# Hybrid decoder layer on one core: token-major x loaded later, 16 columns on another queue, one more filling matmul, and work of the scan and of the attention norm put off

## The chip, the core and the metric

The kernel runs on one core of one Trainium2 chip. The metric is device time in microseconds (us) of one launch. The engines are PE (TensorE: matmuls, and PEld for its weight loads), DVE (VectorE), ACT (ScalarE), POOL (GpSimd) and SP (SyncE, which issues transfers here). Each has its own instruction stream, which it works through in order; they wait for each other through semaphores. SP, ACT and POOL each issue transfers (DMA).

## The reference, cut to what matters

One layer over 256 tokens and a model width of 2048, in float32. `P` stands for the combined input projection.

```python
h = x + 0.5 * swiglu(rmsnorm(x, ffn1_norm), ffn1_w_gu, ffn1_w_down)        # d_ff 5632
P = rmsnorm(h, mix_norm) @ w_in                                            # u | v | z | x | B | C | dt
a = gelu(u) * (tril(w_s) @ rmsnorm(gelu(v)) + b)                           # gated mixing in chunks of 128
x, B, C = split(silu(causal_conv(xBC)));  dt = softplus(dt + dt_bias)
m = ssd_scan(x, dt, -exp(a_log), B, C) + d_skip * x                        # 32 heads of 64, 8 groups, chunk 128
m = rmsnorm(m * silu(z), ssm_norm)
h = h + concat([a, m]) @ w_out
h = h + cross_attention(rmsnorm(h, xa_norm), rmsnorm(mem, mem_norm))       # 4 heads, 256 memory tokens
h = h + 0.5 * swiglu(rmsnorm(h, ffn2_norm), ffn2_w_gu, ffn2_w_down)
out = rmsnorm(h, final_norm)
```

Inside a chunk the scan needs, for each head, `decay[l, s] = exp(cum[l] - cum[s])` for s ≤ l, multiplied by the scores `C @ B`, and that times `x * dt`. `cum` is the running sum of `dt * a`.

## The kernel before, in words

**Products.** Each weight matrix is read once, in pieces of 256 rows by 1024 columns (1 MB, tile `raw`, three buffers, issued by SP). A float32 product is made of three fp32r matmuls: ACT rounds the piece to `hi` (L168, or L190 in quarters for the very first pieces), DVE subtracts to get `lo` (L176), and PE multiplies hi by the activations' high part, lo by the high part and hi by the low part. An ordinary piece (kind C) is 24 matmuls of 128x512; a piece of kind S trades matmuls for sums of blocks (21 matmuls, with further DVE and ACT work). `hi` has three buffers and `lo` two, so `lo` of a piece can be written as soon as the piece two before it has been multiplied.

**Order.** PE's instructions stay in the order in which the program writes them. Other engines' instructions are placed by the framework's scheduler from that program. Side work is put in a list by `later(fn, by)` and runs at a step (L78 to L87): `step()` is called after each piece of weights (in two halves for pieces of kind C), and a job runs at the first step at or after its number, jobs of equal number in the order of the list.

**The start.** The first FFN needs x in two forms: turned (`xt`, features on partitions, tile `turned`, eight loads of 256 KB), which `x_operand` scales by the norm's weights (`col`, whose first 16 columns of 128x244 come early, L113) and splits into operands; and by tokens (`x`, tiles `h0` to `h3`, eight loads of 256 KB by `x_load`, L102), which is the residual stream and from which `Normed.stats` (L491) takes the sum of squares (ACT, `junk`). The factor 1/rms is needed only where the first column block's outputs are scaled (L564), since it scales rows. The first column block goes through its eight pieces in the order 0, 2, 4, 6, 1, 3, 5, 7 (`FIRST`). The pieces 0, 2 and 4 of weights are requested ahead of all, then the turned x, and by `x_operand` (L594) the tokens' x. `keep_busy(4)` puts matmuls on zeros ahead of the first real matmul.

**The scan.** In four parts (two chunks t, two halves j of the heads) `scan_start` (L808) issues the load of `cum` to all partitions (`dec`, 1 MB, POOL's queue) and at once puts down its use: subtraction (L820), minimum against a mask (L821), exponential on ACT (L822), the scores' matmuls, and the multiplication by the scores (L828). `scan_apply` (L832) multiplies by `x * dt` on PE (`yp`) and adds. The parts are called out at steps of the projection v, between its pieces (L875). All this shares twelve large buffers (`slot`).

**The attention norm.** While w_out is added to the stream, `Normed.chunk` puts off the turning of the new stream and the sums of squares (`stats`), the latter by 3 steps. The memory's norm and its turned form are loaded through POOL's queue (`prep_mem`, L966) at the start of w_q.

Of the kernel before, what the change touches and what calls it, by code (L numbers as in the profile page):

```python
# [38 lines left out]
C_FFN1, C_MIX, C_SSM, C_XA, C_MEM, C_FFN2 = (16 * i for i in range(6))  # L39
# [7 lines left out]
def hybrid_layer(ctx: ExitStack, tc: tile.TileContext, x, xt, mem, memt, w_gu1, w_dn1, w_in, w_s, w_out,  # L47
                 w_q, w_kv, w_o, w_gu2, w_dn2, cols, rows, gm_vn, fin, out):
    nc = tc.nc
# [22 lines left out]
    def matmul(out, lhsT, rhs, start=False, stop=False):  # L72
        return pe(nc.tensor.matmul(out, lhsT=lhsT, rhs=rhs, start=start, stop=stop))  # L73
# [4 lines left out]
    def later(fn, by=1):  # L78
        put_off.append((steps[0] + by, len(put_off), fn))
# [9 lines left out]
    def slot(shape, dtype, name):  # L89
        return big.tile(shape, dtype, name=name, tag="slot")  # L90

    def half_k(dtype, name):
        return tmp.tile([P, NC], dtype, name=name, tag="t2k")

    def side(name):
        return mm.tile([P, NC], F32, name=name, tag="bank")
# [5 lines left out]
    def x_load(i, queue=nc.sync):  # L102
        c = i * KP * P
        queue.dma_start(out=h[c // NC][:, :, c % NC:c % NC + KP * P], in_=x_v[:, :, c:c + KP * P])

    def turned_load(w, i, queue, to=None):
        to = half_k(F32, "turned").rearrange("p (k s) -> p k s", k=KP) if to is None else to
        queue.dma_start(out=to, in_=w[i * KP * P:(i + 1) * KP * P, :].rearrange("(k p) s -> p k s", p=P))
        return to

    x_turned = {0: turned_load(xt, 0, nc.scalar)}
    col = const.tile([P, N_COLS], F32, name="col")
    nc.scalar.dma_start(out=col[:, :C_MIX], in_=cols[:, :C_MIX])  # L113
    x_turned[2] = turned_load(xt, 2, nc.scalar)
    warm = const.tile([P, 1], F32, name="warm")
    nc.vector.memset(warm, 0.0)
# [272 lines left out]
    def operand_later(srcs, to, name, c0=None, by=1):  # L389
        def half(q):  # L390
            if q == 0:
                to.append(slot([P, KG, 2 * S], F32R, name))
            return to_operand(srcs, to[at], q, c0)

        at = len(to) + sum(1 for o in owed if o is to)
        owed.append(to)

        def first():
            owed.remove(to)
            assert len(to) == at  # L400
            half(0)
            later(lambda: half(2), by=0)

        later(first, by)
# [4 lines left out]
    class Pieces(dict):  # L409
        def __init__(self, kinds, name, donor=None):  # L410

            self.kinds, self.name, self.half, self.made, self.donor = kinds, name, None, {}, donor
# [57 lines left out]
    class Normed:  # L470


        def __init__(self, name, c0, kinds=None, bys=None):
            self.bys = bys
            self.name, self.c0 = name, c0
            self.xts = [] if kinds is None else Pieces(kinds, f"xp_{name}")
            self.ss = small.tile([P, NT, 4], F32, name=f"ss_{name}", bufs=1)

        def chunk(self, n, by=1):
            srcs = [h[n][:, t, :] for t in range(NT)]  # L480
            if isinstance(self.xts, Pieces):

                for i in (2 * n, 2 * n + 1):
                    later(lambda i=i: self.xts.put(i, srcs, i % 2 * KP, self.c0 + n * KG),
                          self.bys.get(i, by))
                later(lambda: self.stats(n), 3)
            else:
                operand_later(srcs, self.xts, f"xt_{self.name}{n}", self.c0 + n * KG, by)
                self.stats(n)
# [91 lines left out]
    n1 = Normed("ffn1", C_FFN1, GU_KINDS)  # L581
# [11 lines left out]

    def x_operand(i):  # L594
        n1.xts.put(i, x_turned.pop(i), i % 2 * KP, n1.c0 + i // 2 * KG)
        for j in {2: (5,), 4: (7,), 6: (0, 1), 1: (2, 3), 3: (4, 5), 5: (6, 7)}.get(i, ()):
            if j in (5, 7) and i in (2, 4):
                x_turned[j] = turned_load(xt, j, nc.sync)
            else:
                x_load(j)  # L600


    idle = const.tile([P, S], F32, name="idle")
# [2 lines left out]
    def keep_busy(n):  # L606
        ps = side("idle")
        for i in range(n):
            matmul(ps[:, :S], idle[:, :P], idle, start=True, stop=True)

    keep_busy(4)
    x_operand(0)
    for i, by in ((2, 0.5), (4, 1), (6, 1.5), (1, 2), (3, 2.5), (5, 3), (7, 3.5)):
        later(lambda i=i: x_operand(i), by=by)
    for n in range(4):
        later(lambda n=n: n1.stats(n), by=4 + n / 2)

    def late_loads():
        with behind(n1.xts.made[7]):
# [182 lines left out]
    def per_head(ap, n):  # L802
        return ap.unsqueeze(2).broadcast_to([P, ap.shape[1], n])
# [2 lines left out]
    scan = {}  # L806

    def scan_start(t, j):  # L808
        hs = slice(j * 16, j * 16 + 16)
        if j == 0:  # L810
            scan["xdt"] = scan[f"xdt{t}"] = xdt = slot([P, HEADS, HD], F32, "xdt")
            nc.vector.tensor_tensor(out=xdt, in0=y[t], in1=per_head(dt[:, t, :], HD), op=ALU.mult)
            nc.vector.tensor_tensor(out=y[t], in0=y[t], in1=per_head(rowb[:, 2, :], HD), op=ALU.mult)
        dec = slot([P, 16, P], F32, "dec")
        nc.gpsimd.dma_start(
            out=dec.rearrange("p h l -> p (h l)"),
            in_=cum_rows[t:t + 1, j * 16 * P:(j + 1) * 16 * P].broadcast_to([P, 16 * P]))
        if t == 0:
            nc.vector.tensor_tensor(out=dend[:, hs], in0=dec[:, :, P - 1], in1=cum[:, t, hs], op=ALU.subtract)
        nc.vector.tensor_tensor(out=dec, in0=dec, in1=per_head(cum[:, t, hs], P), op=ALU.subtract)  # L820
        nc.vector.tensor_tensor(out=dec, in0=dec, in1=lim.unsqueeze(1).broadcast_to([P, 16, P]), op=ALU.min)  # L821
        nc.scalar.activation(dec, dec, AF.Exp)  # L822
        sc = side("scores").rearrange("p (g l) -> p g l", l=P)
        for i in range(4):
            matmul(sc[:, i, :], bt[:, j * 4 + i, t * P:(t + 1) * P], ctr[:, j * 4 + i, t * P:(t + 1) * P],
                   start=True, stop=True)
        dec4 = dec.rearrange("p (g r) l -> p g r l", r=REP)
        nc.vector.tensor_tensor(out=dec4, in0=dec4, in1=sc.unsqueeze(2).broadcast_to([P, 4, REP, P]),  # L828
                                op=ALU.mult)
        scan["dec"] = dec  # L830

    def scan_apply(t, j):  # L832
        dec, xdt = scan["dec"], scan["xdt"]
        for q in range(2):
            yp = side("yp").rearrange("p (h d) -> p h d", d=HD)
            for i in range(8):
                hh = q * 8 + i
                matmul(yp[:, i, :], dec[:, hh, :], xdt[:, j * 16 + hh, :], start=True, stop=True)
            ys = y[t][:, j * 16 + q * 8:j * 16 + q * 8 + 8, :]
            nc.vector.tensor_tensor(out=ys, in0=yp, in1=ys, op=ALU.add)  # L840
        if j == 0:
            return
        if t == 0:
            nc.scalar.activation(dend, dend, AF.Exp)
            nc.vector.tensor_tensor(out=xdt, in0=xdt, in1=per_head(dend, HD), op=ALU.mult)
            later(scan_states, by=2)
        else:
            for q in range(4):
                yo = side("yo")
                for i in range(2):  # L850
                    g = q * 2 + i
                    matmul(yo[:, i * S:(i + 1) * S], ctr[:, g, P:], scan["states"][:, g, :], start=True, stop=True)
                tq = half_k(F32, "yoff").rearrange("p (h d) -> p h d", d=HD)
                nc.vector.tensor_tensor(out=tq, in0=yo.rearrange("p (h d) -> p h d", d=HD),
                                        in1=per_head(ecum[:, q * 8:q * 8 + 8], HD), op=ALU.mult)
                ys = y[t][:, q * 8:q * 8 + 8, :]
                nc.vector.tensor_tensor(out=ys, in0=ys, in1=tq, op=ALU.add)
# [14 lines left out]
                            base=0, channel_multiplier=-1)  # L872
    v = [slot([P, 4, NC], F32, f"v{t}") for t in range(NT)]
    ss_v = small.tile([P, NT, 4], F32, name="ss_v", bufs=1)
    for i, (by, to) in enumerate(((3, 7), (7, 10), (13, 17), (17, 21))):  # L875
        later(lambda i=i: scan_start(i // 2, i % 2), by=by)
        later(lambda i=i: scan_apply(i // 2, i % 2), by=to)
    for c in (0, 2):
# [69 lines left out]
    for c in range(4):  # L948
        later(lambda c=c: m_operand(c), by=1 + c)
    XA_KINDS = "CCCCCSCS"  # L950
    na = Normed("xa", C_XA, XA_KINDS, {4: 1, 6: 1, 5: 1.5, 7: 2})

    class Both:
        made = {}
# [203 lines left out]
```

## Time and profile before

| what | value |
|---|---|
| median of 3 runs | 2462.12 us (2462.08 to 2463.76) |
| the profiled execution's own time | 2464.31 us |
| its span in the profile | 2462.6 us |
| PE busy | 2442.9 us (99% of the span), 11363 matmuls |
| DVE busy | 2034.9 us (83%) |
| ACT busy | 1311.2 us (53%) |
| mean granted TensorE clock | 0.997 |
| read from memory | 476.76 MB, 194 GB/s over the span |

The profile is of one execution; its own time is 1.7 us above its span. A matmul row's end is modelled and overlaps the next one's start, so what matters on PE is from start to start, and the gap that a row shows in brackets with the engine and line that ended it. In rows of the timeline the columns are start and duration in us, engine, line, operation, output and inputs, shapes, how many; in brackets the idle time ahead of it and what ended that.

### The profile page before, as it was taken

What the parts mean: (1) busy time and instruction counts of PE and PEld (TensorE: products, weight loads), DVE (VectorE), ACT (ScalarE), POOL (GpSimd) and SP (SyncE); (2) the same over time, 40 slices, a digit from 0 to 9 for tenths busy, and PEclk for the clock granted to TensorE, in tenths of its full rate; (3) what the DMA queues carried; (4) which work ended last, traced back from release to release, by engine and by line L of the source; (5) the groups of instructions that cost most, each with busy time, mean ns of one, the idle gap of its engine ahead of it and who ended that gap; (6) DMA issues with size and microseconds to landing.
All of it is one profiled execution on the core that took longest, in us unless ns stands there. A gap on an engine that the chain in (4) does not pass through costs nothing.

```text
span 2462.6 us, 29086 instructions
## 1 busy us (share of the span) xinstructions
PE 2442.9 (99%) x11363; PEld 2035.3 (83%) x11363; DVE 2034.9 (83%) x1936; ACT 1311.2 (53%) x1218; POOL 28.5 (1%) x60
## 2 busy tenths in 40 slices
PE   8999999999999999999999999999999999999998
PEld 6888888888888888788888888888888888888887
DVE  6999889999877778655598888778889988899987
ACT  6555445555546554435555655555555544555554
POOL 0000000000000000000000100000000000000000
PEclk9999999999999999999999999999999999999999
DMA  8555665565656554545556665555555655655664
GB/s 276 188 205 189 205 205 198 197 204 188 205 180 212 193 179 169 198 158 187 184 197 227 222 201 171 171 177 182 188 195 198 205 191 203 205 189 205 200 210 154
DMA packets 202730, 480.80 MB, mean 195 GB/s; under 512 B 15696, under 2 KB 19824, under 8 KB 201824
## 3 DMA queue, kind: packets, MB, share of 16 engines
q1 hardware_dynamic: 199088, 466.41, 56.7%
q0 software_dynamic: 2528, 11.48, 1.3%
q8 instruction: 89, 1.46, 0.2%
q10 hardware_dynamic: 976, 1.06, 0.1%
q14 instruction: 49, 0.40, 0.0%
HBM read 476.76 MB, written 2.13 MB: 194 GB/s over the span
## 4 chain that ended last, share of the span: by engine, by line
PE 95%; issue 3%; ACT 1%; DVE 1%; DMA 0%; POOL 0%; ACTq 0%; SPq 0%; POOLq 0%; DVEq 0%
PE acc L73 91%; PE tpose L76 2%; PE yp L73 1%; PE logits L73 0%; PE o L73 0%; ACT hi L168 0%; DVE lo L176 0%; DMA raw<-in_w_gu 0%; DMA turned<-in_xt 0%; PE mixed L73 0%; ACT junk L352 0%; PE dt L73 0%; PE scores L73 0%; ACT mem L972 0%; PE yo L73 0%
## 5 line engine op out<-in xcount | busy, mean ns | idle before, releaser
L176 DVE TENSOR_TENSOR lo<-raw,hi 128x2048 fp32r<-128x2048 f32 (+2 forms) x446 | 944.5, 2119 | 280.0 <-PE acc L73 220.1
L168 ACT CAST hi<-raw 128x2048 fp32r<-128x2048 f32 (+1 forms) x438 | 787.5, 1799 | 538.0 <-PE acc L73 472.4
L73 PE MATMUL acc<-hi,xp_ffn 128*128 128x512 f32 x1824 | 581.9, 392 | 6.4 <-ACT hi L168 4.4
L73 PEld LDWEIGHTS acc<-hi,xp_ffn 128*128 128x128 f32 x1824 | 344.5, 189 | 78.6 <-ACT hi L168 4.8
L168 ACT CAST hi<-sum 128x2048 fp32r<-128x2048 f32 x117 | 224.3, 1917 | 300.6 <-PE acc L73 169.9
L73 PE MATMUL acc<-lo,xp_ffn 128*128 128x512 f32 x912 | 356.9, 391 | 1.5 <-DVE lo L176 1.5
L176 DVE TENSOR_TENSOR lo<-sum,hi 128x2048 fp32r<-128x2048 f32 x117 | 268.1, 2291 | 32.4 <-ACT hi L168 31.8
L73 PE MATMUL acc<-hi,hid 128*128 128x512 f32 x896 | 282.5, 390 | 0.0
L73 PE MATMUL acc<-hi,xt_mix 128*128 128x512 f32 x768 | 241.7, 393 | 0.0
L73 PEld LDWEIGHTS acc<-lo,xp_ffn 128*128 128x128 f32 x912 | 172.3, 189 | 37.6 <-DVE lo L176 2.5
L538 DVE TENSOR_TENSOR part<-acc,part 128x512 f32<-128x512 f32 x272 | 180.4, 685 | 24.6 <-ACT part L504 9.0
L73 PEld LDWEIGHTS acc<-hi,hid 128*128 128x128 f32 x896 | 168.2, 188 | 34.8
L73 PE MATMUL acc<-lo,hid 128*128 128x512 f32 x448 | 174.3, 389 | 0.0
L73 PEld LDWEIGHTS acc<-hi,xt_mix 128*128 128x128 f32 x768 | 144.2, 188 | 30.4 <-issue 0.7
L176 DVE TENSOR_TENSOR sum<-sum,raw 128x512 f32<-128x512 f32 x234 | 161.5, 690 | 6.6
L73 PE MATMUL acc<-lo,xt_mix 128*128 128x512 f32 x384 | 149.6, 390 | 1.1 <-DVE lo L176 1.1
L73 PE MATMUL acc<-hi,xp_ffn1s 128*128 128x512 f32 x466 | 148.5, 389 | 0.0
L73 PE MATMUL acc<-hi,xp_ffn2s 128*128 128x512 f32 x466 | 148.5, 389 | 0.0
L176 DVE TENSOR_TENSOR sum<-raw 128x1024 f32<-128x1024 f32 x117 | 142.4, 1217 | 0.0
L73 PE MATMUL acc<-xt_mix,hi 128*128 128x512 f32 x512 | 140.5, 396 | 0.0
L73 PE MATMUL acc<-hi,hids 128*128 128x512 f32 x392 | 125.2, 389 | 0.0
L73 PE MATMUL acc<-hi,memt 128*128 128x512 f32 x384 | 123.4, 392 | 0.0
(285 smaller groups left out, 3125.8 us busy)
## 6 DMA issues: line engine op xcount, KB each, us to landing
raw<-in_w_gu SPq DMA_DIRECT2D x286, 512.0 KB, 3.7
raw<-in_w_in SPq DMA_DIRECT2D x80, 1024.0 KB, 5.1
raw<-in_w_dn SPq DMA_DIRECT2D x60, 1024.0 KB, 5.2
raw<-in_w_gu SPq DMA_DIRECT2D x132, 256.0 KB, 3.9
raw<-in_w_kv SPq DMA_DIRECT2D x24, 1024.0 KB, 5.3
raw<-in_w_out SPq DMA_DIRECT2D x21, 1024.0 KB, 5.3
raw<-in_w_dn SPq DMA_DIRECT2D x28, 512.0 KB, 4.0
raw<-in_w_dn SPq DMA_DIRECT2D x56, 256.0 KB, 4.4
```

Source lines behind the costliest of these rows:

```text
L73: return pe(nc.tensor.matmul(out, lhsT=lhsT, rhs=rhs, start=start, stop=stop))
L76: return pe(nc.tensor.transpose(out=out, in_=in_, identity=identity))
L168: last_cast[:] = [nc.scalar.copy(out=t[:, :n], in_=x[:, :n]).ins]
L176: last_split[:] = [nc.vector.tensor_tensor(**kw).ins]
L538: nc.vector.tensor_tensor(out=out, in0=a, in1=b, op=op)
```

## The change

Four things move; nothing that is computed changes.

- The load of the first 16 columns of `col` is issued by SP, ahead of the first weights, and no longer by ACT between the turned loads 0 and 2.
- `x_operand` no longer issues the loads of x by tokens; these are jobs of their own at steps 2, 2.5, ... 5.5, and the sums of squares go from steps 4 to 5.5 to steps 5.5 to 7. `keep_busy` gets a fifth matmul.
- `scan_start` only issues the load of `dec`; what works on it is the new `scan_decay`, put off by 1.5 steps, and `scan_start` and `scan_apply` get new step numbers.
- The attention norm's sums of squares are put off by 8 steps instead of 3.

```diff
     x_turned = {0: turned_load(xt, 0, nc.scalar)}
     col = const.tile([P, N_COLS], F32, name="col")
-    nc.scalar.dma_start(out=col[:, :C_MIX], in_=cols[:, :C_MIX])
+    nc.sync.dma_start(out=col[:, :C_MIX], in_=cols[:, :C_MIX])
     x_turned[2] = turned_load(xt, 2, nc.scalar)
...
-        def __init__(self, name, c0, kinds=None, bys=None):
-            self.bys = bys
+        def __init__(self, name, c0, kinds=None, bys=None, stats_by=3):
+            self.bys, self.stats_by = bys, stats_by
...
-                later(lambda: self.stats(n), 3)
+                later(lambda: self.stats(n), self.stats_by)
...
     def x_operand(i):
         n1.xts.put(i, x_turned.pop(i), i % 2 * KP, n1.c0 + i // 2 * KG)
-        for j in {2: (5,), 4: (7,), 6: (0, 1), 1: (2, 3), 3: (4, 5), 5: (6, 7)}.get(i, ()):
-            if j in (5, 7) and i in (2, 4):
-                x_turned[j] = turned_load(xt, j, nc.sync)
-            else:
-                x_load(j)
+        if i in (2, 4):
+            x_turned[i + 3] = turned_load(xt, i + 3, nc.sync)
...
-    keep_busy(4)
+    keep_busy(5)
     x_operand(0)
     for i, by in ((2, 0.5), (4, 1), (6, 1.5), (1, 2), (3, 2.5), (5, 3), (7, 3.5)):
         later(lambda i=i: x_operand(i), by=by)
+    for i in range(8):
+        later(lambda i=i: x_load(i), by=2 + i / 2)
     for n in range(4):
-        later(lambda n=n: n1.stats(n), by=4 + n / 2)
+        later(lambda n=n: n1.stats(n), by=5.5 + n / 2)
...
     def scan_start(t, j):
-        hs = slice(j * 16, j * 16 + 16)
...
         nc.gpsimd.dma_start(
             out=dec.rearrange("p h l -> p (h l)"),
             in_=cum_rows[t:t + 1, j * 16 * P:(j + 1) * 16 * P].broadcast_to([P, 16 * P]))
+        later(lambda: scan_decay(t, j, dec), by=1.5)
+
+    def scan_decay(t, j, dec):
+        hs = slice(j * 16, j * 16 + 16)
         if t == 0:
...
-    for i, (by, to) in enumerate(((3, 7), (7, 10), (13, 17), (17, 21))):
+    for i, (by, to) in enumerate(((3, 8), (8, 12), (14, 18.5), (18.5, 23))):
...
-    na = Normed("xa", C_XA, XA_KINDS, {4: 1, 6: 1, 5: 1.5, 7: 2})
+    na = Normed("xa", C_XA, XA_KINDS, {4: 1, 6: 1, 5: 1.5, 7: 2}, 8)
```

What this makes of the instruction streams is seen at three places. In the rows, `raw` is a piece of weights as loaded, `h_90` to `h_93` are h0 to h3.

First place, SP's stream at the start, before the change:

```order
L144 DMA raw<-in_w_gu 128x512 x8
L108 DMA turned<-in_xt 128x2x256 x2
L150 DMA raw<-in_w_gu 128x2x512 x2
L108 DMA turned<-in_xt 128x2x256 x4
L104 DMA h_90<-in_x 128x2x256 x2
L104 DMA h_91<-in_x 128x2x256 x2
L104 DMA h_92<-in_x 128x2x256 x2
L104 DMA h_93<-in_x 128x2x256 x2
L150 DMA raw<-in_w_gu 128x2x512 x7
```

The same stream in the changed kernel:

```order
L113 DMA col<-in_cols 128x16
L144 DMA raw<-in_w_gu 128x512 x8
L108 DMA turned<-in_xt 128x2x256 x2
L150 DMA raw<-in_w_gu 128x2x512 x2
L108 DMA turned<-in_xt 128x2x256 x4
L104 DMA h_90<-in_x 128x2x256 x2
L104 DMA h_91<-in_x 128x2x256
L150 DMA raw<-in_w_gu 128x2x512 x2
L104 DMA h_91<-in_x 128x2x256
L104 DMA h_92<-in_x 128x2x256
L150 DMA raw<-in_w_gu 128x2x512 x2
```

The fourth piece of weights (two loads of 512 KB) stood behind eight loads of x and now stands behind three; the columns are SP's first load.

ACT's stream where that fourth piece is cast, before the change:

```order
L453 ACTIVATE forms<-turned,col 128x256 x2
L461 CAST xp_ffn1s<-forms 128x512 x2
L381 ACTIVATE xp_ffn_330<-turned,col 128x256 x2
L352 ACTIVATE junk,ss_ffn_115<-h_90 128x512
L461 CAST xp_ffn1s<-forms 128x512
L352 ACTIVATE junk,ss_ffn_115<-h_90 128x512
L352 ACTIVATE junk,ss_ffn_115<-h_91 128x512 x2
L352 ACTIVATE junk,ss_ffn_115<-h_92 128x512
L168 CAST hi<-raw 128x2048
```

And in the changed kernel:

```order
L453 ACTIVATE forms<-turned,col 128x256 x2
L461 CAST xp_ffn1s<-forms 128x512 x2
L381 ACTIVATE xp_ffn_326<-turned,col 128x256
L168 CAST hi<-raw 128x2048
L461 CAST xp_ffn1s<-forms 128x512
L381 ACTIVATE xp_ffn_326<-turned,col 128x256
L352 ACTIVATE junk,ss_ffn_115<-h_90 128x512 x2
L352 ACTIVATE junk,ss_ffn_115<-h_91 128x512 x2
L168 CAST hi<-raw 128x2048 x2
```

The five sums of squares, the cast of `forms` and the second scaling that stood ahead of this `hi` are behind it now. Four of the eight sums follow at once, the other four come seven casts of weights later.

Second place, DVE's stream around the fourth load of `dec`, before the change (`mixed` and `wn` are the gated mixing's product and its norm weights):

```order
L840 TENSOR_TENSOR y_6159<-yp,y_6159 128x512 x2
L820 TENSOR_TENSOR dec<-dec,cum 128x2048
L901 TENSOR_TENSOR v_6989<-mixed,wn 128x512
L821 TENSOR_TENSOR dec<-dec,sum 128x2048
L901 TENSOR_TENSOR v_6990<-mixed,wn 128x512
L176 TENSOR_TENSOR lo<-raw,hi 128x2048 x2
L828 TENSOR_TENSOR dec<-dec,scores 128x2048
```

And in the changed kernel:

```order
L842 TENSOR_TENSOR y_6160<-yp,y_6160 128x512 x2
L903 TENSOR_TENSOR v_6990<-mixed,wn 128x512
L903 TENSOR_TENSOR v_6991<-mixed,wn 128x512
L822 TENSOR_TENSOR dec<-dec,cum 128x2048
L176 TENSOR_TENSOR lo<-raw,hi 128x2048
L903 TENSOR_TENSOR v_6990<-mixed,wn 128x512
L903 TENSOR_TENSOR v_6991<-mixed,wn 128x512
L823 TENSOR_TENSOR dec<-dec,sum 128x2048
L176 TENSOR_TENSOR lo<-raw,hi 128x2048
L830 TENSOR_TENSOR dec<-dec,scores 128x2048
```

Between the subtraction on the loaded `dec` and its minimum there is now a `lo`, and one more between the minimum and the multiplication.

Third place, ACT's stream where w_q begins, before the change:

```order
L168 CAST hi<-sum 128x2048
L461 CAST xp_xas<-forms 128x512 x2
L352 ACTIVATE junk,ss_xa<-h_92 128x512 x2
L352 ACTIVATE junk,ss_xa<-h_93 128x512 x2
L168 CAST hi<-raw 128x2048
L168 CAST hi<-raw 128x1536
```

And in the changed kernel:

```order
L168 CAST hi<-sum 128x2048
L461 CAST xp_xas<-forms 128x512 x2
L168 CAST hi<-raw 128x2048
L168 CAST hi<-raw 128x1536
L974 ACTIVATE mem_10446,ss_mem<-mem_10446 128x512 x4
```

The four sums of squares of h2 and h3 no longer stand ahead of these two casts; they follow four casts of weights later, behind the memory's own squares.

## The prediction

> **What bounds the kernel now.** I read the page's busy times and chain first, then who PE waited for, then PE's timeline.
>
> ```profile
> span 2462.6 us, 29086 instructions
> PE 95%; issue 3%; ACT 1%; DVE 1%; DMA 0%; POOL 0%; ACTq 0%; SPq 0%; POOLq 0%; DVEq 0%
> PE acc L73 <- ACT hi L168: 4.4, 1, 4.4
> PE acc L73 <- DVE lo L176: 3.5, 4, 1.5
> PE acc L73 <- ACT hi L190: 2.0, 1, 2.0
> ```
>
> The chain is matmuls. All the edits could ever win is PE's waits (total, count, longest): 9.9 us, plus what a low clock costs after them. The timeline says where they lie, with the first matmul of the second operand group (40.04) for the pace:
>
> ```profile
> 25.01 0.39 PE L73 MATMUL acc<-hi,xp_ffn 128*128 128x512 f32 x1
> 29.77 0.80 PE L73 MATMUL acc<-hi,xp_ffn 128*128 128x512 f32 x1 [4.37 <-ACT hi L168]
> 32.09 0.79 PE L73 MATMUL acc<-lo,xp_ffn 128*128 128x512 f32 x1 [1.53 <-DVE lo L176]
> 40.04 0.39 PE L73 MATMUL acc<-hi,xp_ffn1s 128*128 128x512 f32 x1
> 1035.62 0.50 PE L73 MATMUL acc<-lo,xt_mix 128*128 128x512 f32 x1 [1.07 <-DVE lo L176]
> 1403.41 0.50 PE L73 MATMUL acc<-lo,xp_xa 128*128 128x512 f32 x1 [0.39 <-DVE lo L176]
> 67.60 41.50 PE acc L73 x183
> ```
>
> The last row, from the chain of waits, gives the pace at full clock: 41.50 / 183 = 0.2268 us a matmul. PE waits 5.9 us at the start, at the fourth piece of weights; 1.07 us in the scan; and 0.39 us, then 0.52 us at 1410 (quoted below), where w_q begins. The start costs more than its waits: the granted clock (the column ahead of the DMA share) falls.
>
> ```profile
> 27.00:28.00 1.00, 0.00 (x0) 0.00 (x0) 0.00 (x0) 1.00 (x5) 0.20 (x1) 0.72 1.03 381
> 36.00:37.00 1.00, 1.00 (x4) 0.71 (x3) 0.00 (x0) 0.00 (x0) 0.00 (x0) 0.50 0.65 174
> 37.00:38.00 1.00, 1.00 (x5) 0.81 (x4) 0.00 (x0) 0.00 (x0) 0.00 (x0) 0.66 0.84 270
> ```
>
> It goes to one half at 27.44 (0.44 us at 1.0 and 0.56 at 0.5 make 0.72) and back at 37.68. From 32.09 there are 23 matmuls to 40.04: 7.95 us instead of 5.22, so the low clock costs 2.7 us.
>
> **The start, part by part.** The fourth piece is late twice over: it lands late, and then ACT is at the sums of squares.
>
> ```profile
> raw<-in_w_gu SPq DMA_DIRECT2D x1, 512.0 KB, 7.2
> 19.46 12.97 SPq L150 DMA_DIRECT2D raw<-in_w_gu  x6
> 10.00:25.40 15.40, 15.40 (x67) 12.34 (x66) 12.78 (x27) 12.42 (x26) 0.00 (x0) 1.00 1.08 363
> 23.44 0.91 ACT L381 ACTIVATE xp_ffn<-turned,col 128x256 fp32r<-128x256 f32 x2
> 24.25 0.61 ACT L352 ACTIVATE junk<-h 128x512 f32<-128x512 f32 x1
> 27.83 1.88 ACT L168 CAST hi<-raw 128x2048 fp32r<-128x2048 f32 x1
> 29.74 2.29 DVE L176 TENSOR_TENSOR lo<-raw,hi 128x2048 fp32r<-128x2048 f32 x1 [3.45 <-ACT hi L168]
> ```
>
> Its second half is issued at 19.46 and lands 7.2 us later, at 26.7. Transfers run full here, at 363 GB/s, so each 256 KB load ahead costs 0.72 us; five of eight go behind it: 3.6 us, landing at 23.1. On ACT only the first of the two scalings at 23.44 is still ahead, so the cast starts at 23.9 and not at 27.83: 3.9 us earlier, and `lo` follows in the same distance, from 32.09 to 28.15 on PE. The cast, not the landing, sets it; 0.8 us of landing are to spare. SP's new first load costs all others behind it up to one issue (about 0.5 us: SP's eight first loads go 0.47 us apart), most of which the full transfer queue swallows: I take 0.1. **Waits at the start: 3.8 us less** (3.3 to 4.0).
>
> The columns and the filling matmul I cost at nothing:
>
> ```profile
> 5.61 0.91 ACT L381 ACTIVATE xp_ffn<-turned,col 128x256 fp32r<-128x256 f32 x2 [1.82 <-DMA col<-in_cols]
> 1.27 3.78 PE L73 MATMUL idle<-idle 128*128 128x256 f32 x8 [1.27 <-DVE idle L604]
> 7.08 0.79 PE L73 MATMUL acc<-hi,xp_ffn 128*128 128x512 f32 x1 [2.02 <-ACT hi L190]
> 14.98 1.91 ACT L168 CAST hi<-raw 128x2048 fp32r<-128x2048 f32 x1 [1.77 <-DMA raw<-in_w_gu]
> 16.92 2.29 DVE L176 TENSOR_TENSOR lo<-raw,hi 128x2048 fp32r<-128x2048 f32 x1 [2.59 <-ACT hi L168]
> ```
>
> ACT waits for the columns until 5.61; half a microsecond earlier moves PE's start from 7.08 to about 6.5, and one more filling matmul (3.78 / 4 = 0.95 us) fills to 6.0, still ahead of it. But the third piece's `lo`, set by its landing, is done at 19.2, and PE already comes to it at 19.8 (25.24 less 24 matmuls). So PE gains 0.6 us at most, and this only makes it wait longer for the fourth piece. If that cover were gone, the fill would cost up to 0.95 us.
>
> Next late would be the fifth piece: four sums (0.61 us each) now stand between the two casts, so it is cast from 29.2 and its `lo` is done at 33.4, and PE wants it at 28.15 + 5.2 = 33.4. Nothing, or the last of it 1 us. The other four sums stand ahead of the first scaling by 1/rms, in 2.05 us of ACT's idle time:
>
> ```profile
> 59.16 0.72 ACT L564 ACTIVATE part<-part,rstd_ffn 128x512 f32<-128x512 f32 x1 [2.05 <-DVE part L538]
> 65.16 0.74 DVE L567 SCALAR_TENSOR_TENSOR part<-part,rstd_ffn 128x512 f32<-128x512 f32 x1
> 66.57 1.03 PE L76 MATMUL tpose<-ident,part 128*128 128x128 f32 x8
> ```
>
> The scaling comes 1 to 1.7 us later, its last product is done at about 66.6 instead of 65.9, just when PE turns it: 0 to 0.5 us, I take nothing.
>
> **The clock** I bound from both sides. The stretch with almost no matmul shrinks from 25.4 to 32.09 to some 24.7 to 28.15, with one matmul in it. If the half clock still comes at 27.44 and 10.24 us are three equal spans of 3.41, it may end after one span (30.85: 1.35 us lost) or two (34.27: 3.1 us lost), where now 2.7 are: 1.4 us won to 0.4 lost; I take **0.5 us won**. If it never comes, 2.7 are won; that is a rival.
>
> [...]
>
> **The scan.** DVE stood 8 us before an unlanded load, with the next weights' `lo` behind:
>
> ```profile
> 1027.67 2.29 DVE L820 TENSOR_TENSOR dec<-dec,cum 128x2048 f32<-128x2048 f32 x1 [7.96 <-DMA dec<-cum_rows]
> 1033.28 4.48 DVE L176 TENSOR_TENSOR lo<-raw,hi 128x2048 fp32r<-128x2048 f32 x2
> 1019.29 0.53 POOL L815 DMA_DIRECT2D dec<-cum_rows  x1 [3.09 <-PE yp L73]
> DMA to landing us min/median/max: 4.8/6.8/8.4
> 786.96 1.10 POOL L815 DMA_DIRECT2D dec<-cum_rows  x2 [2.71 <-DMA cum_rows<-cumt]
> ```
>
> The fourth load is still released by the part before it; with two pieces (48 matmuls, 10.9 us) and a mixing pair (1.3 us) more ahead, it goes at 1031.5 and lands by 1039.9 at the slowest of the four. Subtraction and `lo`, 2.3 us each, end at 1044.5; PE wants that `lo` at about 1046.9. So DVE may wait again, but with 2.4 us to spare. New is the second load: it went with the first at 787, and in the changed program it waits for the first part's last matmuls (some 957.5), landing by 965.9; subtraction, minimum and `lo` end at 972.8, where PE wants it near 974.8. **1.0 us won** (1.07, to 2 us lost if both margins fail).
>
> **The attention norm.** Four sums hold ACT from 1396.68 to the cast at 1399.14:
>
> ```profile
> 1396.68 0.64 ACT L352 ACTIVATE junk<-h 128x512 f32<-128x512 f32 x1
> 1399.14 3.28 ACT L168 CAST hi<-raw 128x2048 fp32r<-128x2048 f32 x2
> 1401.07 2.29 DVE L176 TENSOR_TENSOR lo<-raw,hi 128x2048 fp32r<-128x2048 f32 x1 [1.44 <-ACT hi L168]
> 1410.35 0.50 PE L73 MATMUL acc<-lo,xp_xas 128*128 128x512 f32 x1 [0.52 <-DVE lo L176]
> 1400.40 5.80 POOL L108 DMA_DIRECT2D memturned<-in_memt  x8
> ```
>
> Casts 2.46 us earlier bring the first `lo` forward by the 1.44 us that DVE waited, and all behind it; both PE waits, 0.39 and 0.52, are shorter. **0.9 us won.** The eight loads of the turned memory also go earlier (their norm no longer stands ahead on POOL), into w_out's stream; w_q's pieces, which they crowd now, gain. Put at nothing; up to 1 us either way.
>
> **The sum:** 3.8 + 0.5 + 1.0 + 0.9 = 6.2 us. The profiled execution took 2464.31 us (span and 1.7 around it), so it becomes 2458.1; the median of the runs shown stands 2.2 below it: 2455.9 us.
>
> **The rivals.**
> 1. *The clock holds at the start.* For it: the stretch without work is half as long. Against it: it fell 2 us after the last matmul. 6.2 + 2.2 = 8.4 won: 2453.7 us.
> 2. *The wait moves to the fifth piece.* For it: no margin in 33.4 against 33.4, and the sums there wait for loads of x that now come behind the fourth piece. Against it: a low clock gives PE more to do meanwhile. Some 1.7 us back: 4.5 won, 2457.6 us.
> 3. *DVE waits for the decay again, with `lo` behind.* For it: a load that was 140 us early now has 2 us. Against it: 8.4 us was the slowest. The 1.0 is lost and 2 us more: 3.2 won, 2458.9 us.
> 4. *Slower: the same place, with loads that take far longer.* Each microsecond past 10.4 (second) and 10.8 (fourth) is one of PE. At 16 us a load that is 10.8 us, against 5.2 won elsewhere: 2467.7 us. It decides from 13.2 us a load; none was over 8.4.
>
> **How the numbers follow.** Forecast 0.48 (2454.5 to 2457.3 by its own bounds), rivals 0.22, 0.12, 0.13 and 0.05. A measurement of this kernel tells 0.2% from no change, 4.9 us, so faster means below 2457.2: most of the forecast (0.43), all of rival 1 and part of rival 2 (0.05) make 0.70; slower is rival 4, 0.05; the rest 0.25. The range leaves a tenth out on either side: from just under rival 1 to past rival 3, 2453.0 to 2459.4.
>
> **What would show it.** Right: the fourth piece cast near 24 with no sum ahead of it, PE's `lo` near 28; a clock that is back by 31 or 34; no PE wait in the scan; none over 0.2 us near 1400. Wrong: a PE wait ahead of the fifth piece, or a wait on a `lo` behind a subtraction of `dec`. The forecast fails as a whole if the fourth piece lands after 24.

## The result, and the profile after

The changed kernel takes 2456.47 us (median of 9 runs, 2454.64 to 2457.30) against 2463.48 us for the kernel before in the same comparison (9 runs, 2462.08 to 2465.49): a ratio of 0.9972, 95% interval 0.9963 to 0.9981. It is faster by 7.0 us. The forecast was 2455.9 us, within 2453.0 to 2459.4.

The page's first line and the answer on whom PE waited for, of the changed kernel (us in total, times, longest):

```profile
span 2454.4 us, 29090 instructions
PE acc L73 <- DVE lo L176: 3.7, 3, 1.8
PE idle L73 <- DVE idle L601: 1.3, 1, 1.3
PE acc L73 <- ACT hi L168: 1.0, 1, 1.0
```

The profiled execution took 2456.08 us, its span 2454.4 (2462.6 before): 8.2 us less. Of PE's waits, 4.7 us are left beside the one ahead of the filling matmuls, and all lie in the first 28 us. PE's timeline, of the third and the fourth piece of weights and of the second operand group's first matmul, and then of the three matmuls in w_q with which operand groups begin:

```profile
18.82 0.50 PE L73 MATMUL acc<-lo,xp_ffn 128*128 128x512 f32 x1 [1.64 <-DVE lo L176]
25.34 0.50 PE L73 MATMUL acc<-hi,xp_ffn 128*128 128x512 f32 x1 [1.00 <-ACT hi L168]
27.67 0.50 PE L73 MATMUL acc<-lo,xp_ffn 128*128 128x512 f32 x1 [1.82 <-DVE lo L176]
34.62 0.39 PE L73 MATMUL acc<-hi,xp_ffn1s 128*128 128x512 f32 x1
1395.95 0.39 PE L73 MATMUL acc<-hi,xp_xa 128*128 128x512 f32 x1
1401.39 0.39 PE L73 MATMUL acc<-hi,xp_xas 128*128 128x512 f32 x1
1406.15 0.39 PE L73 MATMUL acc<-hi,xp_xa 128*128 128x512 f32 x1
```

The same three in the kernel before:

```profile
1402.64 0.39 PE L73 MATMUL acc<-hi,xp_xa 128*128 128x512 f32 x1
1408.76 0.39 PE L73 MATMUL acc<-hi,xp_xas 128*128 128x512 f32 x1
1414.34 0.39 PE L73 MATMUL acc<-hi,xp_xa 128*128 128x512 f32 x1
```

Setting equal matmuls of the two traces side by side gives the whole account:

| stage | how read | won, us |
|---|---|---|
| start, waits | `lo` of the fourth piece: 32.09 to 27.67 | 4.42 |
| start, clock | from there to the second group: 7.95 to 6.95 | 1.00 |
| scan | the lead grows from 5.42 (at 40) to 6.68 (at 1079) | 1.26 |
| attention norm | 6.12 to 5.44 between the first two rows, 5.58 to 4.76 between the next | 1.50 |
| sum | | 8.2 |

That is the difference of the two profiled executions. The execution before took 0.83 us more than its median, the one after 0.39 less than its own: 8.23 - 0.83 - 0.39 = 7.0, the difference of the medians.

### The profile page after: what moved, and what is told of

Same layout as the page of the kernel before. It is cut to its first block, busy times and chain, and to the rows that moved or that the text cites. A ratio compares the mean times of both kernels' runs of the same rounds, so it can differ in the third digit from the quotient of the medians.

```text
span 2454.4 us, 29090 instructions
## 1 busy us (share of the span) xinstructions
PE 2439.9 (99%) x11365; PEld 2034.0 (83%) x11365; DVE 2035.8 (83%) x1936; ACT 1311.5 (53%) x1218; POOL 27.5 (1%) x60
## 4 chain that ended last, share of the span: by engine, by line
PE 96%; issue 3%; DMA 0%; ACT 0%; DVE 0%; SPq 0%; POOL 0%; POOLq 0%; DVEq 0%; ACTq 0%
PE acc L73 91%; PE tpose L76 2%; PE yp L73 1%; DMA raw<-in_w_gu 0%; PE o L73 0%; PE logits L73 0%; PE mixed L73 0%; PE dt L73 0%; ACT hi L168 0%; PE scores L73 0%; PE yo L73 0%; PE st L73 0%; DVE lo L176 0%; DVE h L1105 0%; ACT xp_ffn1s L461 0%
```

## The experiments

For each kernel: its median, its ratio to the kernel before with interval, and from its one profile the time of PE's first matmul of the second operand group (40.04 before, 34.62 after) and the time at the half clock (without that at the end of each profile).

| kernel | us (runs) | ratio | second group | half clock, us |
|---|---|---|---|---|
| before (with start only to x by tokens last) | 2463.05 (27) | | 40.04 | 10.24 |
| changed | 2456.47 (9) | 0.9972 (0.9963 to 0.9981) | 34.62 | 3.41 |
| start only | 2458.43 (11) | 0.9982 (0.9973 to 0.9990) | 34.96 | 3.41 |
| columns and fill only | 2462.50 (10) | 0.9998 (0.9989 to 1.0007) | 39.13 | 6.83 |
| loads of x only | 2457.00 (10) | 0.9978 (0.9969 to 0.9987) | 34.53 | 3.41 |
| x by tokens last | 2453.23 (5) | 0.9961 (0.9948 to 0.9975) | 31.47 | none |
| scan only | 2462.32 (10) | 0.9997 (0.9988 to 1.0007) | 39.62 | 6.83 |
| attention norm only | 2461.52 (10) | 0.9994 (0.9985 to 1.0004) | 39.34 | 3.41 and 6.83 |
| fill in the gaps | 2454.87 (5) | 0.9967 (0.9954 to 0.9980) | 33.42 | none |
| fill in one gap | 2454.89 (5) | 0.9969 (0.9957 to 0.9982) | 34.30 | 3.41 |
| decay load slowed | 2454.43 (1) | | 32.91 | none |
| operands later | 2453.27 (4) | 0.9961 (0.9946 to 0.9977) | 30.70 | none |
| all in order of need | 2452.45 (5) | 0.9958 (0.9946 to 0.9971) | 28.91 | none |
| x behind the sixth piece | 2453.88 (5) | 0.9966 (0.9952 to 0.9979) | 29.16 | none |

The medians of the three parts differ from before by 4.6, 0.6 and 1.4 us, 6.7 in all against 7.0 for the whole change. For the scan and the norm alone the interval holds no change, so those two are read from the traces. The kernels were measured in several comparisons, in which the kernel before has medians of 2462.28 to 2463.48 us: a difference between two kernels of different comparisons is uncertain by about a microsecond, and each ratio is taken within its own.

### The start alone

The edit is the change without its edits to `scan_start` and to `na`.

> The kernel before with the edits of the start alone (columns on SP in front, one more filling matmul, loads of x and their sums of squares put off). Theory, the parts add up and each acts in its own stage: PE comes to its second operand group at 34.6 us as in the changed kernel (40.0 before), the waits in the scan (1.07) and at the attention norm (0.39, 0.52) stay, and the execution is 5.4 us shorter than the kernel before. By the terms of the prediction it would be 4.3 us. Rival, the parts depend on each other (the scan's or the norm's wait shrinks or grows when the start moves): PE's waits after 40 us sum to another figure than 1.98 us.

PE's second group starts at 34.96 and the waits at the attention norm stay (0.39 and 0.48). But the wait in the scan, which this kernel does not touch, is another than in the execution before:

```profile
1022.13 2.29 DVE L819 TENSOR_TENSOR dec<-dec,cum 128x2048 f32<-128x2048 f32 x1 [7.50 <-DMA dec<-cum_rows]
1030.08 0.50 PE L73 MATMUL acc<-lo,xt_mix 128*128 128x512 f32 x1 [0.61 <-DVE lo L176]
```

PE waits after 40 us 1.48 and not 1.98 us in all. That need not be the start acting on the scan: with the attention norm alone (below), whose start is that of before, PE has no wait there at all.

### Columns and fill, and the loads of x, each alone

```diff
-    nc.scalar.dma_start(out=col[:, :C_MIX], in_=cols[:, :C_MIX])
+    nc.sync.dma_start(out=col[:, :C_MIX], in_=cols[:, :C_MIX])
-    keep_busy(4)
+    keep_busy(5)
```

> The kernel before with the columns as SP's first load and the fifth filling matmul, nothing else. The prediction's theory: PE starts its first real matmul near 5.3 instead of 7.08 us, and the fourth piece of weights, whose cast on ACT sets it, takes that back: its cast starts at 27.4 to 27.8 as before, and the execution is 0 to 0.5 us shorter. Rival: the earlier columns are worth what PE starts earlier, 1.8 us.

PE's timeline of this kernel, the first real matmul and the fourth piece; then DVE's at the fourth load of the decay:

```profile
5.21 0.50 PE L73 MATMUL acc<-hi,xp_ffn 128*128 128x512 f32 x1
29.87 0.79 PE L73 MATMUL acc<-hi,xp_ffn 128*128 128x512 f32 x1 [4.99 <-ACT hi L168]
32.20 0.79 PE L73 MATMUL acc<-lo,xp_ffn 128*128 128x512 f32 x1 [1.53 <-DVE lo L176]
1025.75 2.29 DVE L820 TENSOR_TENSOR dec<-dec,cum 128x2048 f32<-128x2048 f32 x1 [6.95 <-DMA dec<-cum_rows]
```

PE starts 1.87 us earlier (7.08 before), three times the 0.6 that the prediction gave it, and comes to the fourth piece's `lo` at 32.20 (32.09 before): all of it is lost there. The rival falls. (The columns and the fill were not tried apart.) The lead of 0.9 us at the second group is the clock's (6.83 us low in place of 10.24). In the scan there is no wait at all.

```diff
-        for j in {2: (5,), 4: (7,), 6: (0, 1), 1: (2, 3), 3: (4, 5), 5: (6, 7)}.get(i, ()):
...
+    for i in range(8):
+        later(lambda i=i: x_load(i), by=2 + i / 2)
```

> The kernel before with the loads of x put off, nothing else (the sums of squares keep their places by step, the columns theirs). Theory, the fourth piece's landing and the sums that wait for x follow from the loads alone: its cast starts near 23.9 instead of 27.83 with no sum ahead of it, PE's last wait ends near 28.1, and the start is 4.5 to 5.0 us shorter, nearly all that the start edits give together. Rival, the sums of squares that are not put off stand ahead of the fifth and sixth pieces' casts and give some of it back: a wait of PE of 1 us or more between 33 and 45 us.

ACT's timeline and PE's:

```profile
22.88 0.51 ACT L381 ACTIVATE xp_ffn<-turned,col 128x256 fp32r<-128x256 f32 x1
23.30 1.89 ACT L168 CAST hi<-raw 128x2048 fp32r<-128x2048 f32 x1
27.57 0.59 PE L73 MATMUL acc<-lo,xp_ffn 128*128 128x512 f32 x1 [1.82 <-DVE lo L176]
```

The loads alone give the start: `lo` at 27.57 without the columns, the fill or the sums put off, where the changed kernel has 27.67. The sums that stay ahead of later casts cost PE no wait. Start only is 1.4 us above this in the medians, but where the record gives a run the same mean clock the two are alike: 2456.56 and 2456.78 us on average at 0.999, 2458.94 and 2458.75 at 0.998. The difference lies in how many runs had the lower one, four of ten here and nine of eleven there; whether the other start edits change those odds is not shown by so few.

Five profiles have the scan as it was. DVE stood before the load for 7.96 (before), 7.50, 7.16 (loads of x only), 6.95 and 6.89 us (attention norm only), and PE then waited 1.07, 0.61, 0.27, 0 and 0. So PE waits for what DVE's wait has over 6.9 us, and DVE's wait for the load varies by 1.07 us over these five executions. The wait that the change removes is worth 0 to some 1.3 us; the profile before had the largest of the five draws.

### The scan alone, the attention norm alone

> The kernel before with the decay's work put off behind its load, nothing else. Theory: the 1.07 us wait at 1035.6 goes and nothing takes its place; with the refill of PE's pipeline after a wait that is 1.2 to 1.3 us of the span. The waits at the start (4.37, 1.53) and at the attention norm (0.39, 0.52) stay. Rival 3 of the prediction: a wait of PE on a lo behind a subtraction of dec, between 955 and 1060.

> The kernel before with the attention norm's squares put off to step 8, nothing else. Theory: the two waits at 1403 and 1410 (0.39, 0.52) go, and the span is 1.5 us shorter, more than their 0.91, since each wait also drains and refills PE's pipeline (0.27 to 0.3 us each between the pace of 0.227 us and the row's durations). By the prediction's terms it is 0.9. Rival: the loads of the turned memory, which now go earlier into the stream of w_out, give a wait of up to 1 us there.

Neither kernel has a wait left in its own stage, and neither got a new one. What the norm's two waits were worth is seen best in the two stretches of w_q in the first section: the brackets of the kernel before have 0.39 and 0.52, what was won is 0.68 and 0.82, about 0.30 us more a wait. The bracket counts from the modelled end of the last matmul (its row has 0.39 us, while matmuls follow each other in 0.227), and the first matmul after a wait is longer (0.50).

### The clock: filled gaps

```diff
+                if m < len(fills) and fills[m]:
+                    keep_busy(fills[m])
                 matmul(banks[name], ...)
...
+    FILLS = {3: (1, 2)}        # in the second kernel {3: (0, 1)}
```

Fill in the gaps:

> The changed kernel with three more filling matmuls on zeros (0.95 us each): one ahead of the fourth piece's first hi, two ahead of its first lo, where PE waits 1.0 and 1.8 us. Theory, the clock falls where a span of 3.41 us holds too little matmul work (34% here): with the gaps filled it stays at 1.0 through 45 us, the 17 or so matmuls of the slow span run at 0.227 us, and the execution is 1.5 to 1.7 us shorter than the changed kernel. Rival, the clock answers to something else (the waits themselves, or transfers): it falls all the same and the time is the same or up to 0.4 us longer, by what the fill overshoots.

Fill in one gap:

> The changed kernel with one filling matmul of 0.95 us ahead of the fourth piece's first lo, so that some 60% of the span of 3.41 us is work. Theory, a share decides and lies between 40% (fell in the kernel before) and this: the clock stays, 1.5 us shorter than the changed kernel. Rival, the clock needs the span nearly full: it falls near 28 and the time is that of the changed kernel.

With both gaps filled the clock stays at 1.0 in the profile, and the five runs, all with a recorded mean clock of 0.999, lie within 0.6 us (2454.50 to 2455.08), where the nine of the changed kernel spread over 2.7. With one filled, the clock fell in the profiled run for 3.41 us all the same; its median is that of both filled, but its runs spread over 2.2 us (2454.47 to 2456.64). The share of work that I had worked out for that was wrong, because it assumed where the span begins. The windows view of the changed kernel, of the kernel before, of the norm alone and of one gap filled, cut in each where its clock changes and at multiples of 3.41 us from there (columns: window, its length, then busy us of PE, PEld, DVE, ACT and POOL, then the clock, DMA share and GB/s):

```profile
24.93:28.34 3.41, 1.17 (x4) 0.78 (x5) 3.02 (x3) 3.41 (x10) 0.00 (x0) 1.00 1.07 370
28.34:31.75 3.41, 3.41 (x10) 2.64 (x9) 1.91 (x4) 2.90 (x4) 1.27 (x2) 0.50 1.08 380
```

```profile
24.03:27.44 3.41, 1.37 (x7) 0.79 (x5) 2.27 (x7) 3.41 (x11) 1.28 (x2) 1.00 1.04 386
27.44:30.85 3.41, 0.80 (x1) 0.29 (x1) 1.11 (x1) 3.41 (x7) 0.00 (x0) 0.50 1.06 387
30.85:34.27 3.42, 2.18 (x5) 1.80 (x6) 2.31 (x4) 3.42 (x6) 0.72 (x1) 0.50 0.46 119
34.27:37.68 3.41, 3.41 (x9) 2.63 (x9) 1.41 (x1) 0.89 (x1) 0.00 (x0) 0.50 0.87 287
```

```profile
5.77:9.18 3.41, 1.81 (x7) 1.25 (x8) 2.93 (x6) 3.41 (x8) 0.00 (x0) 1.00 1.03 377
9.18:12.58 3.40, 3.40 (x10) 2.66 (x9) 3.40 (x8) 3.40 (x8) 0.00 (x0) 0.50 1.07 372
```

```profile
16.92:20.33 3.41, 2.17 (x10) 1.46 (x9) 3.41 (x7) 2.32 (x5) 0.00 (x0) 1.00 1.09 364
23.75:27.16 3.41, 1.49 (x6) 0.62 (x4) 2.60 (x4) 3.41 (x6) 0.00 (x0) 1.00 1.06 373
27.16:30.57 3.41, 2.97 (x7) 2.39 (x8) 1.90 (x6) 3.23 (x7) 1.28 (x2) 0.50 1.06 380
```

Read the first number after the comma, PE's busy time, against 3.41. In the eight profiles with a low clock at the start it fell there after nine such spans, with PE busy for 0.00 (columns and fill), 0.18 (norm alone, the second fall), 0.37 (scan alone), 1.17, 1.37, 1.49, 1.54 (the start alone), 1.59 (loads alone) and 1.81 us (0 to 53%), and not after two that had 2.17 (above) and 2.19 us (the start alone), 64%. Once low, it stayed low in these profiles after spans with 0.79 to 2.18 us and came back after 2.97 to 3.41. Two early spans do not fit: in the kernel before and in that with the loads alone, one between 3.5 and 7.4 us had 1.50 and 1.45 us of work and the clock stayed. All of it but one matmul was the filling matmuls on zeros; why they differ is open.

The first fall came at 9.18 to 30.00 us in these eight profiles, and what the same gaps cost differs with where the spans lie. The clearest case is a kernel made for something else, the slowed decay load (below), whose program is the same up to the scan:

```profile
25.24 0.49 PE L73 MATMUL acc<-hi,xp_ffn 128*128 128x512 f32 x1 [1.01 <-ACT hi L168]
27.56 0.50 PE L73 MATMUL acc<-lo,xp_ffn 128*128 128x512 f32 x1 [1.83 <-DVE lo L176]
32.91 0.39 PE L73 MATMUL acc<-hi,xp_ffn1s 128*128 128x512 f32 x1
28.00:29.00 1.00, 1.00 (x6) 0.82 (x5) 0.88 (x4) 1.00 (x3) 0.00 (x0) 1.00 1.06 391
```

The same waits as in the changed kernel's profile (1.00, 1.82), yet no low clock, and the second group at 32.91 in place of 34.62: 1.71 us, half of one span of 3.41. So the fill gains nothing over such an execution (2454.43 us, against a median of 2454.87 with both gaps filled); what it changes is the draw, as far as its five runs show.

Where the spans lay in this execution is estimated from its end. The profiles before, of the changed kernel and of this one also end at the half clock, when PE has no work left. In the first two this last fall comes a whole number of the same spans after the first one: with 10.24 / 3 = 3.4133 us a span, 712 before (27.44 and 2457.72) and 709 in the changed kernel (28.34 and 2448.39). With the slowed load it comes at 2449.21, which is 710 spans after 25.75:

```profile
22.33:25.75 3.42, 2.39 (x10) 1.42 (x8) 2.61 (x6) 3.42 (x6) 0.00 (x0) 1.00 1.06 375
25.75:29.16 3.41, 1.60 (x7) 1.34 (x8) 3.13 (x5) 3.41 (x10) 0.08 (x1) 1.00 1.08 373
2449.21:2450.21 1.00, 0.00 (x0) 0.00 (x0) 0.00 (x0) 0.00 (x0) 0.00 (x0) 0.50 1.03 379
```

Each of these spans takes one of the two waits (2.39 and 1.60 us of work), where in the changed kernel's profile one span takes the second wait and part of the first (1.17). But 1.60 us, 47%, is no more than the 1.59 after which the clock fell with the loads alone, and less than the 1.81 after which it fell with the norm alone. So the spans after which it fell are those with less work for the most part, but in these profiles no single share parts the two cases.

### Where the start's loads stand

x by tokens last: steps 3.5 to 5.25 in place of 2 to 5.5.

> The changed kernel with the loads of x put off further, to the steps 3.5 to 5.25, so that the fourth piece's two loads are issued ahead of all of them. Theory, in the changed kernel the landing at 22.4 us sets the place that the fourth piece's cast gets in ACT's stream, and with the loads in front it lands near 20.3, is cast about 3 us earlier, PE waits for its hi no more and for its lo about 0.4 us in place of 1.0 and 1.8, and the granted clock does not fall: 4.5 us less than the changed kernel. The prediction's statement, that the cast and not the landing sets it: the cast stays at 23.4 and the time is the same within 0.3 us. Rival, the wait moves to the fifth piece, which now has the loads of x in front: a wait of 1 us or more at its first matmuls, and half of the gain is lost.

The fourth piece's two issues and how long they took to land, by 20.2 the later one (22.4 in the changed kernel); and ACT's, DVE's and PE's timelines:

```profile
L150 SPq DMA_DIRECT2D raw<-in_w_gu x2: 368/368/368, 11.1 to 11.8; - x2
DMA to landing us min/median/max: 7.8/8.1/8.4
```

```profile
21.85 1.90 ACT L168 CAST hi<-raw 128x2048 fp32r<-128x2048 f32 x1
23.77 2.29 DVE L176 TENSOR_TENSOR lo<-raw,hi 128x2048 fp32r<-128x2048 f32 x1 [0.70 <-ACT hi L168]
26.12 0.50 PE L73 MATMUL acc<-lo,xp_ffn 128*128 128x512 f32 x1 [1.51 <-DVE lo L176]
31.47 0.39 PE L73 MATMUL acc<-hi,xp_ffn1s 128*128 128x512 f32 x1
```

3.2 us faster than the changed kernel, runs 2453.03 to 2453.58. With a landing 2.2 us earlier the cast is 1.55 us earlier, and it has an earlier place in ACT's stream; half of the gain is the clock, which held (5.35 us from the fourth piece's `lo` to the second group, 6.95 in the changed kernel). The rival's wait at the fifth piece does not show. The expected 4.5 is missed because ACT still makes the next pieces' operands first.

Operands later: the same, with the operands of the fifth to eighth pieces at steps 3.5 to 5 in place of 2 to 3.5.

> The kernel in which only x by tokens is put behind the fourth piece, and here also the operands of the fifth to eighth pieces are made later (steps 3.5 to 5 instead of 2 to 3.5). Theory, with the fourth piece landed near 20.2, its cast waits now for the work on those operands (21.85) and its lo for theirs on DVE (23.77): the lo is done some 1.2 us earlier, PE waits 0.3 us there in place of 1.51, and the time is 1.2 to 1.5 us shorter than 2453.2. Rival, the landing of the fifth or sixth piece (31.8) takes it back: a wait there, time the same.

The `lo` comes 0.77 us earlier (25.35), a wait of 0.33 us turns up at 43.41, and the time is the same. The rival holds for the time, though the new wait is at the seventh piece and not at the fifth or sixth.

All in order of need: both of these, the fourth piece requested right behind the third, and x by tokens at steps 4.25 to 5.65.

```diff
     for i in (4, 6):
         x_turned[i] = turned_load(xt, i, nc.sync)
-    first_load(4)
+        first_load(i)
```

> The changed kernel with the loads at the start put in the order in which PE needs them: behind the third piece comes the operand's sixth load and the fourth piece at once, then the other four loads of x by features, the fifth piece, then x by tokens (steps 4.25 to 5.65), and the operands of the later pieces are made a piece later (steps 3.5 to 5). Theory, what PE waits for at the start is the order of the transfers alone, which run full: third piece 0.7 us earlier, fourth landed near 17.5 and its lo done near 22.5, before PE comes to it at 23.8, no low clock; PE's second operand group starts near 28.0 (34.6 in the changed kernel, 31.5 with only x by tokens put back), some 2450 us. Rival, the wait moves on to the fifth or sixth piece, whose operands and casts now stand late on ACT and DVE: a wait of 1 us or more between 28 and 45 us, and a time no better than the run with only x by tokens put back, 2453.2 us.

```profile
35.27 0.50 PE L73 MATMUL acc<-lo,xp_ffn1s 128*128 128x512 f32 x1 [0.54 <-DVE lo L176]
42.62 0.50 PE L73 MATMUL acc<-lo,xp_ffn1s 128*128 128x512 f32 x1 [0.89 <-DVE lo L176]
```

PE comes to the second group at 28.91, 2.6 us before the kernel with x by tokens last, and then gives 2 us back at the sixth and seventh pieces. The theory's 2450 us is missed by that; the waits are of the rival's kind, but each is under its 1 us, and the time is 0.8 us below that with x by tokens last. It is the fastest of all kernels: 2452.45 us, 4.0 below the changed kernel (3.4, each taken against its own comparison), with no run in common.

x behind the sixth piece: the same, x by tokens at steps 5.25 to 6.1 and the sums at 6.25 to 7.

> The kernel with all loads of the start in the order of need, with x by tokens put off further: its eight loads go behind the sixth piece's (steps 5.25 to 6.1), and all eight sums of squares are taken together at the end of the first chunk (steps 6.25 to 7). Theory: there, PE's waits of 0.54 and 0.90 us at the sixth and seventh pieces (35.3 and 42.6 us, each with 0.3 us of refill) came from three sums of squares ahead of the sixth piece's cast (30.98) and from loads of x ahead of the seventh's; both go, and the time is 2 us shorter, 2450.4. Rival, the eight sums (0.61 us each) now hold ACT ahead of the first scaling by 1/rms and PE waits for the pieces it turns there: a wait of 1 us or more between 50 and 62 us, and a time of 2452 or more.

```profile
56.69 1.33 ACT L564 ACTIVATE part<-part,rstd_ffn 128x512 f32<-128x512 f32 x2 [3.18 <-POOL rstd_ffn L360]
58.25 0.33 PE L76 MATMUL tpose<-ident,part 128*128 128x128 f32 x1 [1.43 <-DVE part L567]
58.91 0.33 PE L76 MATMUL tpose<-ident,part 128*128 128x128 f32 x1 [0.33 <-DVE part L567]
```

The rival holds: the wait at the sixth piece goes and that at the seventh is still 0.69 us, but 1/rms is late for the first scaling, and PE waits 1.43 and 0.33 us for what it turns there. It is 1.4 us slower (2.0, each against its own comparison). The last sum ends 1.6 us later than in the kernel with all in order of need; DVE is then at a `lo` and adds them up at 54.06 instead of 51.49. So the sums of squares are free in their places only because they end early enough.

### The decay's margin

```diff
+        if t == 1 and j == 1:
+            for _ in range(5):
+                nc.gpsimd.memset(dec, 0.0)
         nc.gpsimd.dma_start(
```

> The changed kernel with five memsets of dec on POOL ahead of the fourth load of the decay rows, some 9 to 10 us that only put off that load. The changed kernel's trace has a margin of 5.4 us there (lo done at 1038.0, PE at its first matmul at 1043.4). Theory (rival 4's mechanism of the prediction): DVE stands before the load with the weights' lo behind it, PE waits at that lo for what the delay exceeds the margin, 3.5 to 4.6 us for 9 to 10 us, and the execution is that much longer. Rival, the scheduler's order leaves enough lo ahead: no wait of PE over 1 us.

In the changed kernel DVE waited 4.74 us for this load, and the `lo` behind was done at 1038.0, 5.4 us before PE came to it:

```profile
1033.51 2.29 DVE L822 TENSOR_TENSOR dec<-dec,cum 128x2048 f32<-128x2048 f32 x1 [4.74 <-DMA dec<-cum_rows]
1035.72 2.29 DVE L176 TENSOR_TENSOR lo<-raw,hi 128x2048 fp32r<-128x2048 f32 x1
1043.41 0.40 PE L73 MATMUL acc<-lo,xt_mix 128*128 128x512 f32 x1
```

With the load put off by five memsets (9.27 us on POOL), so that it lands 8.1 us later, DVE's timeline has another order:

```profile
1038.67 2.29 DVE L176 TENSOR_TENSOR lo<-raw,hi 128x2048 fp32r<-128x2048 f32 x1 [3.71 <-issue]
1041.64 2.29 DVE L825 TENSOR_TENSOR dec<-dec,cum 128x2048 f32<-128x2048 f32 x1 [0.68 <-DMA dec<-cum_rows]
```

No wait on PE: with the memsets in the program the scheduler put the `lo` ahead of the subtraction. So this prices no late load in an unchanged order; that was not tried otherwise, and rival 4's price stays an argument.

## Why the prediction was right

- **The fourth piece.** Forecast: cast at 23.9, `lo` on PE at 28.15, waits 3.8 us less. Measured 23.40, 27.67 and 4.42. The mechanism was right, and one edit, the loads, does it. That the cast sets it, not the landing, is half right. It holds for the order of this stream (landed at 22.4, cast at 23.40, right behind the operand's scaling); but with the loads requested earlier the scheduler makes another order and the cast comes 1.55 us earlier, as x by tokens last shows.
- **Columns and fill at nothing.** Right; the cover named (the wait for the fourth piece) took all of 1.87 us. Part of it is now a wait of 1.64 us at the third piece's `lo`, not one of the waits foreseen.
- **The fifth piece at 33.4 against 33.4 (rival 2).** There is no wait. ACT casts it at 28.57, `lo` is done at 32.77, and PE comes to it at 34.84. Of these 2 us the low clock gave 1.7, so the margin is 0.4 where the clock holds, and there was no wait there in such runs either.
- **The clock, 0.5 won, bounds 1.4 won to 0.4 lost.** Measured 1.00, within, but that is one execution's draw. The forecast and rival 1 are not two answers, of which one is true: a low clock and none are both seen with one program up to the scan (the changed kernel, and the slowed load). That the 10.24 us before are three equal spans was an assumption of the forecast; the stretches measured at the start since, 3.41, 6.83 and 10.24 us, are one, two and three times 3.41. It also took the spans to lie where they lay before (27.44); in the changed kernel's profile the fall came 0.9 us later (28.34), and in the execution with the slowed load the spans lay, by the estimate from its end, so that each of the two waits fell into another one and the clock held. The gaps alone do not tell the cases apart: the clock fell with gaps of 1.00 and 1.82 us on PE in the changed kernel's profile, and it held with 1.01 and 1.83 us with the slowed load.
- **The scan, 1.0 won.** Measured 1.26 against the profile before, but this was that execution's draw; by the five profiles the wait was 0.39 us on average (1.95 / 5), so 1.0 was too much. Rivals 3 and 4 did not come: the second load cost PE nothing and the fourth had 5.4 us to spare, where the forecast had 2.4 at the slowest load.
- **The attention norm, 0.9 won.** The term that was mis-sized: 1.5. The two waits were priced at their brackets; each costs 0.3 us more. The loads of the turned memory, put at nothing, cost nothing.
- **The first scaling by 1/rms, nothing.** Right, and where its cover ends is now known: with all eight sums in one place PE waits 1.76 us there.
- **The sum.** 6.2 forecast, 8.2 between the two profiles, 7.0 between the medians. Too little for the waits at the start and in the norm and too much for the scan; these errors partly cancelled. More was won than forecast, and yet the median came 0.6 us above the forecast: that was counted from a median of 2462.12 us, and in the comparison the kernel before took 2463.48. So that the time came this close is in part luck.

## What to carry to other kernels

When the start is bound by transfers (370 GB/s from 24.93 to 28.34 us in the changed kernel, while PE waited), list what each wait needs and request in that order: putting off loads that nothing needs yet gave 5.5 us here, and going on with it 3.4 to 4 more, until the next wait (1/rms) set the end. A wait seen in one profile is one draw where a load (6.89 to 7.96 us of DVE's wait before the same load here) or the clock (3.41 us at one half, or none) is behind it; look for the same wait in the profiles of kernels that leave the place alone before pricing its removal. And price a wait on PE from start to start of the matmuls around it, not by its bracket (0.68 and 0.82 us here, with brackets of 0.39 and 0.52).

## What the runs showed of the hardware that was not expected

- At the start the half clock came in stretches of 3.41, 6.83 and 10.24 us, at another time in each of eight profiles (the first fall at 9.18 to 30.00 us). In spans of 3.41 us counted from the clock's changes, it fell after nine with 0.00 to 1.81 us of matmul work and held after those with 2.17 and 2.19 and, with the slowed load, 2.39 and 1.60 us; once low it stayed low after 0.79 to 2.18 us and came back after 2.97 to 3.41. The two early spans with filling matmuls (1.50 us before, 1.45 with the loads alone; held) are the exception. PE's wait ahead of its first real matmul, 2.02 us, was followed by no low clock until 27.44 us in the profile before; with the same start, in the profile of the attention norm alone (2.09 us there), 3.41 us of half clock followed at 9.18.
- That draw is much of a kernel's spread: 2.7 to 4.1 us between the fastest and slowest run of the changed kernel, of the start alone and of the loads alone, and 0.5 to 0.7 us for four kernels whose profile shows no low clock (fill in the gaps, x by tokens last, operands later, all in order of need). In a fifth, x behind the sixth piece, one of five runs lies 1.5 us apart, and it alone has a recorded mean clock of 0.998 in place of 0.999. With the loads alone the six runs at 0.999 took 2455.83 to 2457.06 us and the four at 0.998 took 2457.96 to 2459.92. The changed kernel's nine do not part so: its fastest, 2454.64, has 0.998.
- DVE's wait for the fourth load of `dec`, 1 MB through POOL's queue, ran from 6.89 to 7.96 us in five executions in which the scan's order is the same.
